# Second expert group's gates made first, groups of 76 and 52, and first-stage products kept in PSUM banks

## The chip, the cores and the metric

One NeuronCore of one Trainium2 chip runs the kernel in one launch. The metric is device time of that launch in microseconds. Engines are called as the profile calls them: PE multiplies matrices, DVE and ACT work on tiles of up to 128 partitions, POOL does the same more slowly, SP issues the loads. "mmb" and "msb" are PSUM banks (128 x 512 f32), everything else lies in SBUF.

## What is computed

Two transformer blocks over 256 tokens of width 1024, all in f32. The first block is a pair of convolution mixers, a cross-attention to 256 memory rows, and a layer of 16384 small experts; the second is attention and an MLP. The change concerns the mixers and the experts:

```
sc_b, sc_c, sc_x, cf_a, cf_g, gate_sc, gate_cf = jnp.split(h @ w_in, cuts)
y_sc = sc_b * causal_depthwise_conv(sc_c * sc_x, sc_conv_w)     # 3 taps
cf   = causal_depthwise_conv((cf_a + b) * sigmoid(cf_g + b), cf_conv_w)  # 31 taps
...
top_s, top_i = lax.top_k(sub_scores, 16)          # 8 heads, two halves of 128 keys
cand = top_s[0][:, None] + top_s[1][None, :]      # 256 candidates
fin_s, fin_pos = lax.top_k(cand, 16)              # 16 experts of each head
gates = softmax(fin_s)
act = gelu(u[expert] . h) * gates
out = sum over experts of act * v[expert]
```

## The kernel before

Activations lie transposed (features on partitions, 256 tokens along a row). f32 precision comes from splitting: every weight tile `w` (128 x 1024, 512 KB, loaded by SP into one of three buffers) is split by ACT into `wh` (L288) and by POOL or DVE into `wl` = w - wh (L292), and a **unit** is 24 matmuls of 128 x 256 (L370): `wh` with the high and the low part of the activation, `wl` with the high part. What follows a unit (`post_...`) reads its mmb bank.

The order on all engines comes from a planner, `Sched`, at build time. Work is written as generators of `Op(engine, cost, fn, deps, ev)`; the planner keeps a clock for each engine, adds each `Op`'s planned cost, and emits what is due while it walks the units in PE's order. `sch.need(events)` emits work until the events are planned. An engine runs its queue in that order, so a cost in the table moves instructions and a `need` puts what follows behind what it asked for.

The stages around the change:

- **First stage** (0 to about 290 us): units of `w_in` in columns a, g (the 31-tap mixer `cf`) and c, x, b (the 3-tap mixer `sc`). DVE runs `cf`'s taps with one SCALAR_TENSOR_TENSOR each (L607, accumulating in an msb bank). `post_x` makes the 3-tap filter: `scx` = x * c (L238), then one TENSOR_SCALAR (L659) and two SCALAR_TENSOR_TENSORs (L662) in the SBUF tile `scy`; `post_b` multiplies `scy` into b's bank and splits the result into `eA`, `eB`, the activations of later units. `prep_n` and `prep_mem` make the normalised `hN` and `memHL` over an SBUF tile `mt` (L238, L479).
- **U**: 128 units of `peer_u`; unit n's 128 experts are multiplied with h. `post_u` writes gelu to `Ah[n // 64][:, n % 64]` (L1239, ACT).
- **Choice**: during the first third of U, `topk_head` and then `select(t)` for the two halves of 128 tokens run on DVE. In `select`, four quarters of is_equal, multiply and reduce (L1179, L1182, L1185) turn positions to expert numbers; three PE transposes (L1192), ACT copies (L1196, L1200) and two DVE operations (L1201, L1203) give `sel`: for each of a token's 128 chosen experts the unit number i (0 to 127), the row j in the unit and the gate g.
- **Gates**: `gbatch(hh, t0)` makes the gates of 8 tokens for one group `hh` of units. DVE: J (L1255, is_equal, 128 x 1024 f16), I (L1259, is_equal, 8 tokens x 64 units), T (L1262, I times g in two parts). PE: 8 matmuls J x T (L1274) into two msb banks. For each bank, ACT copies the low part out (L1284), DVE adds it (L1286) and multiplies the sum into `Ah[hh]` (L1288). Two lanes take 16 batches each (`gate_lane`). Group 0 (units 0 to 63) runs during units 64 to 127; group 1 during the first half of V.
- **V**: 128 units of `peer_v`, in the order 0 to 127, accumulated in four msb banks (L1362, L1364, L1366). `z_split` turns gated activations into `zz`: high part by ACT (L241), low part by DVE (L238); it needs all 32 batches of the unit's group. At V's 72nd unit the rope angles of the second block are spawned on DVE (`angles`, `distances`).

Of the kernel before, what the change touches and what calls it, by code (L numbers as in the profile page):

```python
# [200 lines left out]
def tile_kernel(ctx, tc, A, out):  # L201
# [449 lines left out]
    def post_x(j):  # L651
        def g(p):
# [32 lines left out]
    def prep_n(k):  # L685
        t = T1.tile([128, S], F32, tag="mt", bufs=2, name="mt")
# [18 lines left out]
    def layer_norm():  # L705
# [122 lines left out]
    for key, j in order:  # L828
        u_in[key, j] = add(W["w_in"][tiles0[key] + j])
# [19 lines left out]
    u_V = [add(W["peer_v"][n]) for n in range(128)]  # L849
# [288 lines left out]
    def top16(val, idx, src, tmp, n, ev=None, deps=()):  # L1138
        yield Op("dve", c_dve(n), lambda: V.max(val[:, 0:8], src), deps=deps)
        yield Op("dve", c_dve(n), lambda: V.max_index(idx[:, 0:8], val[:, 0:8], src), chain=False)  # L1140
        yield Op("dve", c_dve(n), lambda: V.match_replace(tmp, val[:, 0:8], src, LOW), chain=False)
        yield Op("dve", c_dve(n), lambda: V.max(val[:, 8:16], tmp))
        yield Op("dve", c_dve(n), lambda: V.max_index(idx[:, 8:16], val[:, 8:16], tmp), ev=ev)

    def topk_head(h):
        for t in range(2):
# [9 lines left out]
    def select(t):  # L1156
# [14 lines left out]
        yield Op("dve", c_dve(128), lambda: V.tensor_scalar(FQ[:, 0], fp, 4, None, op0=OP.logical_shift_right))  # L1171
        yield Op("dve", c_dve(128), lambda: V.tensor_copy(AFi[:, t], FQ[:, 0]))
        yield Op("dve", c_dve(128), lambda: V.tensor_scalar(FQ[:, 1], fp, 15, None, op0=OP.bitwise_and))
        yield Op("dve", c_dve(128), lambda: V.tensor_copy(BFi[:, t], FQ[:, 1]))
        for q, (pos, dst) in enumerate(((AFi, IF), (BFi, JF))):
            for c in range(2):
                eq = EQ[c].rearrange("p (s r) -> p s r", r=16)
                eq4 = EQ[c].rearrange("p (h s r) -> p h s r", h=4, r=16)
# [953 lines left out]
```

## Time and profile before

| | |
|---|---|
| runs | 1784.63, 1784.19, 1780.41 us; median 1784.19 |
| profiled execution | 1783.02 us, span 1781.2 us, 1.8 us around it |
| busy share of the span | PE 90%, PEld 89%, DVE 76%, POOL 68%, ACT 47% |
| granted TensorE clock, mean | 0.951 |

The span runs from the first to the last instruction. Busy shares are means over stages that differ, so the stretches below are read one by one. A clock of 1.00 is 2.4 GHz, 0.50 is 1.2 GHz. In a wait, the engine named first sat idle until the instruction after the arrow ended.

### The profile page before, as it was taken

How to read it: one execution, taken by the hardware profiler on the slowest of the kernel's cores; microseconds unless marked ns; L12 is line 12 of the kernel's file. 1: busy time of each engine (PE TensorE's matmuls, PEld its weight loads, DVE VectorE, ACT ScalarE, POOL GpSimd, SP SyncE). 2: the span in 40 equal slices, each digit the busy share in tenths (PEclk: the TensorE clock that was granted, in tenths of full speed). 3: DMA queues.
4: the chain of work that ended last, by engine and by line, in shares of the span. 5: the costliest groups of instructions: out<-in, count | busy, mean ns of one | idle time of the engine just before them, and what ended most of it. 6: DMA issues, size and time to landing. Idle time of an engine off the chain costs nothing. (4 is left out here: it accounts for less than half of the span.)

```text
span 1781.2 us, 32465 instructions
## 1 busy us (share of the span) xinstructions
PE 1605.8 (90%) x12948; PEld 1579.4 (89%) x12948; DVE 1362.3 (76%) x2122; ACT 839.0 (47%) x1431; POOL 1210.3 (68%) x509
## 2 busy tenths in 40 slices
PE   8898988898997899999988888878999889979997
PEld 7898988898997899999888888878999779979997
DVE  7999966758899805999999999978887886464302
ACT  5533445555443444444444334333455455556533
POOL 5677865546687787777766666646887533758885
PEclk8999999999998999999999989988999899989999
DMA  5444544434354354444443434333555322535553
GB/s 202 155 166 154 193 155 140 154 125 151 134 187 154 119 189 151 158 145 156 157 153 131 137 118 142 138 108 137 179 187 169 119 80 72 179 129 179 188 185 113
DMA packets 75304, 266.69 MB, mean 150 GB/s; under 512 B 8720, under 2 KB 9232, under 8 KB 75152
## 3 DMA queue, kind: packets, MB, share of 16 engines
q1 hardware_dynamic: 73856, 262.77, 43.3%
q8 instruction: 101, 1.65, 0.4%
q10 hardware_dynamic: 1296, 1.85, 0.3%
q14 instruction: 51, 0.42, 0.1%
HBM read 262.48 MB, written 2.10 MB: 149 GB/s over the span
## 5 line engine op out<-in xcount | busy, mean ns | idle before, releaser
L292 POOL TENSOR_TENSOR wl<-w,wh 128x1024 fp32r<-128x1024 f32 x473 | 1186.6, 2514 | 539.8 <-ACT wh L288 437.5
L288 ACT ACTIVATE wh<-w 128x1024 fp32r<-128x1024 f32 x491 | 518.2, 1058 | 499.0 <-PE mmb L370 152.6
L1364 PE MATMUL msb<-zz,wh 128*128 128x256 f32 x1008 | 260.0, 293 | 6.9 <-DVE zz L238 6.8
L1362 PE MATMUL msb<-zz,wh 128*128 128x256 f32 x1008 | 260.8, 293 | 3.0 <-ACT zz L241 3.0
L370 PE MATMUL mmb<-hA,wh 128*128 128x256 f32 x1024 | 256.9, 288 | 0.0
L370 PE MATMUL mmb<-hB,wh 128*128 128x256 f32 x1024 | 254.9, 286 | 0.0
L238 DVE TENSOR_TENSOR zz<-Ah,zz 128x256 fp32r<-128x256 f32 x128 | 215.8, 1689 | 35.1 <-ACT zz L241 35.1
L1364 PEld LDWEIGHTS msb<-zz,wh 128*128 128x128 f32 x1008 | 203.6, 202 | 8.1 <-DVE zz L238 8.1
L1362 PEld LDWEIGHTS msb<-zz,wh 128*128 128x128 f32 x1008 | 203.6, 202 | 3.4 <-ACT zz L241 3.4
L370 PEld LDWEIGHTS mmb<-hA,wh 128*128 128x128 f32 x1024 | 199.4, 195 | 0.0
L370 PEld LDWEIGHTS mmb<-hB,wh 128*128 128x128 f32 x1024 | 199.2, 195 | 0.0
L1366 PE MATMUL msb<-zz,wl 128*128 128x256 f32 x1008 | 149.1, 292 | 0.0
L370 PE MATMUL mmb<-hA,wl 128*128 128x256 f32 x1024 | 146.3, 286 | 0.0
L1366 PEld LDWEIGHTS msb<-zz,wl 128*128 128x128 f32 x1008 | 135.8, 200 | 0.0
L370 PEld LDWEIGHTS mmb<-hA,wl 128*128 128x128 f32 x1024 | 133.2, 193 | 0.0
L370 PE MATMUL mmb<-hN,wh 128*128 128x256 f32 x896 | 118.7, 284 | 12.7 <-ACT hN L241 5.5
L370 PEld LDWEIGHTS mmb<-hN,wh 128*128 128x128 f32 x896 | 111.9, 194 | 14.5 <-ACT wh L288 5.9
L607 DVE SCALAR_TENSOR_TENSOR msb<-glu,vec,msb 128x256 f32<-128x256 f32 x232 | 113.0, 487 | 6.2
L1274 PEld LDWEIGHTS <-ohF 128*128 128x128 f16 x512 | 38.7, 151 | 71.3 <-DVE selT L1262 41.3
L1259 DVE TENSOR_TENSOR ohF<-selT 128x512 f16<-128x512 f16 x64 | 98.9, 1545 | 0.0
L1255 DVE TENSOR_TENSOR ohF<-selT 128x1024 f16<-128x1024 f16 x64 | 80.9, 1265 | 0.0
L1262 DVE TENSOR_TENSOR ohF<-ohF,selT 128x1024 f16<-128x1024 f16 x32 | 79.1, 2473 | 0.1
(478 smaller groups left out, 3285.7 us busy)
## 6 DMA issues: line engine op xcount, KB each, us to landing
w<-in_peer_u_dram SPq DMA_DIRECT2D x128, 512.0 KB, 3.2
w<-in_peer_v_dram SPq DMA_DIRECT2D x128, 512.0 KB, 3.2
w<-in_w_in_dram SPq DMA_DIRECT2D x81, 512.0 KB, 3.3
w<-in_w_up_dram SPq DMA_DIRECT2D x32, 512.0 KB, 3.7
w<-in_w_down_dram SPq DMA_DIRECT2D x32, 512.0 KB, 4.3
w<-in_w_peer_q_dram SPq DMA_DIRECT2D x16, 512.0 KB, 3.5
w<-in_w_v_dram SPq DMA_DIRECT2D x8, 512.0 KB, 3.2
w<-in_sc_w_out_dram SPq DMA_DIRECT2D x8, 512.0 KB, 4.3
```

The lines of the kernel that those rows point to most:

```text
L238: return lambda e="dve": ENG[e].tensor_tensor(o, a, b, op=op)
L288: yield Op("act", c_act(1024), lambda: ACT.activation(h, w, AF.Copy), deps=u["wdep"], ev=("H", u["i"]))
L292: lambda e: ENG[e].tensor_tensor(l, w, h.bitcast(F32), op=OP.subtract), ev=("L", u["i"]))
L370: PE.matmul(p[:, :S], a, b, start=first and n == 0, stop=last and n == len(todo) - 1)
L607: lambda k=k: V.scalar_tensor_tensor(cc[:, j] if k == 30 else o(), glu[:, j, k:k + S], vcol("cf_w", j * 31 + k), o(), op0=OP.mult, op1=OP. ...
L1255: yield Op("dve", G_J, lambda: V.tensor_tensor(ohJ, iotax, sel["j"][:, None, sl].to_broadcast([128, 128, 8]), op=OP.is_equal), deps=[("sel ...
L1259: yield Op("dve", G_I, lambda: V.tensor_tensor(ohI, iotan[:, None, hh * 64:(hh + 1) * 64].to_broadcast([128, 8, 64]), sel["i"][:, sl][:, : ...
L1262: yield Op("dve", G_T, lambda: V.tensor_tensor(gT, ohI[:, :, None].to_broadcast([128, 8, 2, 64]), sel["g"][:, :, sl].rearrange("p a t -> p ...
L1274: PE.matmul(banks[c][:, t * 128:(t + 1) * 128], ohJ[:, :, 4 * c + t], gT[:, 4 * c + t], start=True, stop=True, skip_group_check=True)
L1362: PE.matmul(o, u["H"][:, d, :], opH, start=first and d % 2 == 0, stop=False, skip_group_check=True)
L1364: PE.matmul(o, u["H"][:, d, :], opL, start=False, stop=False, skip_group_check=True)
L1366: PE.matmul(o, u["L"][:, d, :], opH, start=False, stop=last, skip_group_check=True)
```

## The change

Three things, in one diff of some 500 lines.

**Groups.** The units are split 76 and 52. The gates of group 1 (units 76 to 127) are made first, as soon as both halves of `sel` are planned and at the latest before unit 48; they need no activation, so one DVE addition stores them in `Ah[1]` (L1328 of the new kernel). From unit 76 on, `post_u` runs gelu in the bank and one DVE operation multiplies it with the kept gate (L1264). Before unit 76, `sch.need` asks for all of group 1's batches; then group 0's start, in chunks of 3, 3 and 2 tokens. V takes units 76 to 127 first, then 0 to 75. Between the start of the gates and unit 76, the `wl` splits are held on DVE by a bias (units 51 to 75). Banks for gates rotate over four.

**First stage.** `prep_n`, `prep_mem` and the first two steps of the 3-tap filter write into PSUM banks; only the last tap writes SBUF. The `wl` of all `w_in` tiles are held on POOL.

**Costs.** The planner's costs of DVE operations on SBUF rise by 1050 ns in `select`, `z_split` and the angles (`c_wait`), and some other costs are set to other numbers.

```diff
+def c_wait(n, ap=0, fast=False):
+
+    return 1050 + c_dve(n, ap, fast)
...
     def prep_mem(k):
-        t = T1.tile([128, S], F32, tag="mt", bufs=2, name="mt")
+        t = prep_bank[k % 2]()[:, :S]
...
-            yield Op("dve", c_dve(S), tt(b[:, 2:2 + S], p[:, :S], scc[j], OP.mult), deps=[("scc", j)])
-            yield Op("dve", c_dve(S, 1, True),
-                     lambda: V.tensor_scalar(y, b[:, 0:S], vcol("sc_w", j * 3), None, op0=OP.mult))
+
+            o = p[:, :S]
+            yield Op("dve", c_psum(S), tt(b[:, 2:2 + S], o, scc[j], OP.mult), deps=[("scc", j)])
+            yield Op("dve", c_psum(S, 2),
+                     lambda: V.tensor_scalar(o, b[:, 0:S], vcol("sc_w", j * 3), None, op0=OP.mult))
             for k in (1, 2):
-                yield Op("dve", c_dve(S, 1),
-                         lambda k=k: V.scalar_tensor_tensor(y, b[:, k:k + S], vcol("sc_w", j * 3 + k), y,
-                                                            op0=OP.mult, op1=OP.add),
+                yield Op("dve", c_psum(S, 1),
+                         lambda k=k: V.scalar_tensor_tensor(y if k == 2 else o, b[:, k:k + S],
+                                                            vcol("sc_w", j * 3 + k), o, op0=OP.mult, op1=OP.add),
                          ev=("scy", j) if k == 2 else None)
...
-        u_in[key, j] = add(W["w_in"][tiles0[key] + j])
+        u_in[key, j] = add(W["w_in"][tiles0[key] + j], bias=-1e6)
...
+    NG = (76, 52)
+    vord = list(range(NG[0], 128)) + list(range(NG[0]))
+    u_V = [add(W["peer_v"][n]) for n in vord]
...
     def post_u(n):
+        g_, m = place(n)
+
         def g(p):
-            yield Op("act", c_act(S), lambda: ACT.activation(Ah[n // 64][:, n % 64], p[:, :S], AF.Gelu),
-                     ev=("U", n))
+            if g_ == 0:
+                yield Op("act", c_act(S), lambda: ACT.activation(Ah[0][:, m], p[:, :S], AF.Gelu), ev=("U", n))
+                return
+
+            a, z = p[:, :S], Ah[1][:, m]
+            yield Op("act", c_act(S), lambda: ACT.activation(a, a, AF.Gelu))
+            yield Op("dve", c_psum(S), lambda: V.scalar_tensor_tensor(
+                z, a, 1.0 / GS, z, op0=OP.mult, op1=OP.mult), deps=[("Z", 1, 240), ("Z", 1, 248)], ev=("U", n))
...
+    def gbank(key):
+
+        if len(gbanks) >= 4:
+            sch.need([gbanks[-4]])
+        gbanks.append(key)
+        return gpool[0]()
...
+        chunks = [(t, min(per, 8 - t)) for t in range(0, 8, per)]
...
+            if hh == 1:
+                yield Op("dve", c_psum(nt * NI), lambda view=view, lc=lc, z=z: V.tensor_tensor(
+                    z, view(0), lc, op=OP.add), deps=[("Ga", hh, t0, c)], chain=False, ev=("Zc", hh, t0, c))
+                continue
...
-        if n == 64:
-            sch.need([("U", 62), ("sel", 0), ("sel", 1)])
-            Ah[1] = P2.tile([128, 64, S], F32, tag="A1", name="Ah1")
+        if Ah[1] is None and (n == 48 or n > 4 and ("sel", 0) in sch.ev and ("sel", 1) in sch.ev):
+            sch.need([("sel", 0), ("sel", 1)])
+            Ah[1] = P2.tile([128, NG[1], S], F32, tag="A1", name="Ah1")
             ohF[0] = epool.tile([128, 4096], HF, tag="e0a", name="ohF")
-            sch.need([("U", 63)])
-            gates_half(0, msb)
+            ACT.activation(iotan(), iota, AF.Copy)
+            gates_group(1)
+
+            for k in range(n + 3, NG[0]):
+                u_U[k]["bias"] = 1e6
+        if n == NG[0]:
+            sch.need([("U", NG[0] - 1)] + [("Z", 1, t0) for t0 in range(0, 256, 8)])
+            gates_group(0)
...
-        if n == 72:
+        if n == NG[1] + 4:
```

In the first stage, DVE's order around one filter of the 3-tap mixer reads before:

```order
L607 SCALAR_TENSOR_TENSOR msb<-glu,vec,msb 128x256 x6
L238 TENSOR_TENSOR scx<-mmb,scc 128x256
L659 TENSOR_SCALAR scy<-scx,vec 128x256
L607 SCALAR_TENSOR_TENSOR msb<-glu,vec,msb 128x256
L662 SCALAR_TENSOR_TENSOR scy<-scx,vec,scy 128x256
L607 SCALAR_TENSOR_TENSOR msb<-glu,vec,msb 128x256
L662 SCALAR_TENSOR_TENSOR scy<-scx,vec,scy 128x256
L238 TENSOR_TENSOR mmb<-mmb,scy 128x256
```

and now, with the bank of x (mmb) as the place of the running sum:

```order
L620 SCALAR_TENSOR_TENSOR msb<-glu,vec,msb 128x256 x6
L248 TENSOR_TENSOR scx<-mmb,scc 128x256
L674 TENSOR_SCALAR mmb<-scx,vec 128x256
L677 SCALAR_TENSOR_TENSOR mmb<-scx,vec,mmb 128x256
L620 SCALAR_TENSOR_TENSOR msb<-glu,vec,msb 128x256
L677 SCALAR_TENSOR_TENSOR scy<-scx,vec,mmb 128x256
L248 TENSOR_TENSOR mmb<-mmb,scy 128x256
```

The three filter operations are the same, on other operands; a tap of the other mixer (L607, now L620) has moved out from between the first and the second.

In U, PE's order at the first half's transposes of `select` (L1192) reads before, after 33 units (the second half's follow in the same way after 42.67 units):

```order
L370 MATMUL mmb<-hA,wh 128x256
L370 MATMUL mmb<-hB,wh 128x256
L370 MATMUL mmb<-hA,wl 128x256 x8
L1192 MATMUL msb<-cst,scr 128x128 x3
L370 MATMUL mmb<-hA,wh 128x256
L370 MATMUL mmb<-hB,wh 128x256
```

and now, after 48 units:

```order
L380 MATMUL mmb<-hA,wh 128x256
L380 MATMUL mmb<-hB,wh 128x256
L380 MATMUL mmb<-hA,wl 128x256 x8
L1210 MATMUL msb<-cst,scr 128x128 x6
L380 MATMUL mmb<-hA,wh 128x256
L380 MATMUL mmb<-hB,wh 128x256
```

Both halves' transposes now stand behind unit 47 with no unit between them. On DVE the second half's chain stands behind the first half's last two operations (L1219, L1221, which read the transposes), as before:

```order
L1200 TENSOR_TENSOR scr<-scr 128x1024
L1203 TENSOR_REDUCE scr<-scr 128x64
L1219 SCALAR_TENSOR_TENSOR scr<-msb,selT 128x128
L1221 CAST selT<-scr 128x128
L1179 TENSOR_TENSOR scr<-scr 128x128
L1183 TENSOR_REDUCE scr<-scr 128x8
L1184 RECIPROCAL scr<-scr 128x8
```

Behind it on DVE come group 1's batches, the first ones among the `wl` splits of units 51 to 75 (L302; J is L1294, I L1298, T L1301, the addition into `Ah` L1328):

```order
L1221 CAST selT<-scr 128x128
L1294 TENSOR_TENSOR ohF<-selT 128x1024
L302 TENSOR_TENSOR wl<-w,wh 128x1024
L1298 TENSOR_TENSOR ohF<-ohF,selT 128x416
L1294 TENSOR_TENSOR ohF<-selT 128x1024
L302 TENSOR_TENSOR wl<-w,wh 128x1024
L1301 TENSOR_TENSOR ohF<-ohF,selT 128x832
L302 TENSOR_TENSOR wl<-w,wh 128x1024
L1298 TENSOR_TENSOR ohF<-ohF,selT 128x416
L302 TENSOR_TENSOR wl<-w,wh 128x1024
L1328 TENSOR_TENSOR Ah_7162<-msb,hT 128x52x4 x2
L1301 TENSOR_TENSOR selT<-ohF,selT 128x832
```

The last `wl` on DVE belongs to unit 75. Then batch follows batch with no unit's work between, as in these rows:

```order
L1301 TENSOR_TENSOR ohF<-ohF,selT 128x832
L1294 TENSOR_TENSOR ohF<-selT 128x1024
L1298 TENSOR_TENSOR ohF<-ohF,selT 128x416
L1328 TENSOR_TENSOR Ah_7162<-msb,hT 128x52x4 x2
L1301 TENSOR_TENSOR selT<-ohF,selT 128x832
L1294 TENSOR_TENSOR ohF<-selT 128x1024
L1298 TENSOR_TENSOR ohF<-ohF,selT 128x416
L1328 TENSOR_TENSOR Ah_7162<-msb,accp 128x52x4
L1301 TENSOR_TENSOR ohF<-ohF,selT 128x832
L1328 TENSOR_TENSOR Ah_7162<-msb,selT 128x52x4
```

Eleven of the 32 batches have their matmuls on PE between units 52 and 76; those of the other 21 (168 matmuls) stand in one piece after unit 75, ahead of unit 76. Of group 0's batches 20 have their matmuls between units 78 and 126, one where U ends, 10 in V's units 2 to 26. Before, each half of U and V had 32 batches spread over 60 units.

## Rows read from the trace of the kernel before

**Rows 1.** Stretches: length, busy us and instructions of each engine, PEclk, DMA share, GB/s.
```profile
88.80:186.50 97.70, 88.92 (x736) 85.94 (x736) 91.45 (x166) 38.53 (x54) 74.36 (x39) 1.00 0.48 162
474.80:633.60 158.80, 141.71 (x1155) 141.02 (x1154) 139.08 (x357) 70.73 (x109) 126.04 (x47) 0.95 0.46 158
633.60:679.70 46.10, 46.10 (x387) 46.10 (x386) 0.00 (x0) 21.34 (x34) 37.48 (x16) 1.00 0.54 184
723.30:900.20 176.90, 164.38 (x1432) 161.21 (x1432) 171.78 (x181) 83.34 (x156) 135.93 (x51) 1.00 0.44 152
900.60:1172.40 271.80, 221.95 (x1793) 216.77 (x1793) 262.42 (x289) 107.50 (x194) 170.34 (x65) 0.91 0.38 132
1160.00:1172.40 12.40, 3.25 (x25) 2.51 (x25) 10.77 (x22) 2.80 (x8) 0.00 (x0) 0.50 0.11 40
1172.40:1177.00 4.60, 4.60 (x20) 4.43 (x21) 1.38 (x4) 1.35 (x4) 0.00 (x0) 0.50 0.00 0
1172.40:1363.80 191.40, 184.96 (x1478) 184.38 (x1479) 157.82 (x103) 87.56 (x129) 145.66 (x61) 0.95 0.48 164
```

**Rows 2.** Waits of PE over the span: us in total, times, longest.
```profile
PE mmb L1274 <- DVE selT L1262: 34.4, 13, 4.9
PE msb L1192 <- DVE scr L1185: 17.1, 3, 9.7
...
PE mmb L370 <- ACT wh L288: 7.1, 6, 2.2
```

**Rows 3.** Timeline of PE at two first-stage waits: start, length, idle before, releaser.
```profile
154.66 2.10 PE L370 MATMUL mmb<-hN,wh 128*128 128x256 f32 x16 [1.13 <-ACT wh L288]
...
164.92 2.15 PE L370 MATMUL mmb<-hN,wh 128*128 128x256 f32 x16 [1.16 <-ACT wh L288]
```

**Rows 4.** DVE groups, 0 to 230: count, busy us, mean ns, idle before.
```profile
L607 DVE SCALAR_TENSOR_TENSOR msb<-glu,vec,msb 128x256 f32<-128x256 f32 x214 | 104.3, 487 | 5.9
L662 DVE SCALAR_TENSOR_TENSOR scy<-scx,vec,scy 128x256 f32<-128x256 f32 x16 | 19.8, 1240 | 0.0
L659 DVE TENSOR_SCALAR scy<-scx,vec 128x256 f32<-128x256 f32 x8 | 11.5, 1436 | 0.9
...
L603 DVE TENSOR_SCALAR msb<-glu,vec 128x256 f32<-128x256 f32 x8 | 4.4, 546 | 0.3
...
L717 DVE TENSOR_TENSOR msb<-cc 128x256 f32<-128x256 f32 x1 | 1.4, 1402 | 0.0
```

**Rows 5.** Timeline of DVE in a quarter of select.
```profile
577.60 1.23 DVE L1182 TENSOR_TENSOR scr<-scr 128x1024 f32<-128x1024 f32 x1
```

**Rows 6.** Timeline of DVE in the last gate batches.
```profile
1160.05 1.21 DVE L1262 TENSOR_TENSOR selT<-ohF,selT 128x1024 f16<-128x1024 f16 x1
...
1161.52 0.67 DVE L1255 TENSOR_TENSOR ohF<-selT 128x1024 f16<-128x1024 f16 x1
...
1162.75 0.68 DVE L1259 TENSOR_TENSOR ohF<-selT 128x512 f16<-128x512 f16 x1
1163.35 0.42 DVE L1288 SCALAR_TENSOR_TENSOR Ah<-mmb,Ah 128x256 f32<-128x256 f32 x1
...
1167.82 1.21 DVE L1262 TENSOR_TENSOR selT<-ohF,selT 128x1024 f16<-128x1024 f16 x1
```

**Rows 7.** DVE groups, 707 to 900, gates beside POOL's splits.
```profile
L1255 DVE TENSOR_TENSOR ohF<-selT 128x1024 f16<-128x1024 f16 x27 | 44.7, 1657 | 0.0
L1259 DVE TENSOR_TENSOR ohF<-selT 128x512 f16<-128x512 f16 x27 | 43.1, 1596 | 0.0
L1262 DVE TENSOR_TENSOR ohF<-ohF,selT 128x1024 f16<-128x1024 f16 x13 | 42.0, 3230 | 0.0
...
L1262 DVE TENSOR_TENSOR selT<-ohF,selT 128x1024 f16<-128x1024 f16 x14 | 19.0, 1358 | 0.5
```

**Rows 8.** POOL's splits in the same stretch.
```profile
L292 POOL TENSOR_TENSOR wl<-w,wh 128x1024 fp32r<-128x1024 f32 x56 | 148.9, 2659 | 49.5 <-ACT wh L288 49.2 <-DMA w<-in_peer_u_dram 0.3
```

**Rows 9.** DVE group of the lo part of zz, 900 to 1172.
```profile
L238 DVE TENSOR_TENSOR zz<-Ah,zz 128x256 fp32r<-128x256 f32 x64 | 84.2, 1317 | 3.3 <-ACT zz L241 3.3
```

More of the change, by code (lines that the diff above doesn't have):

```diff
@@ L80, in __init__ @@
         self.cos = []
+        self.busy = []
     def spawn(self, gen, prio=0.0, ready=None):
@@ L109, in emit @@
         op = co.op
+        self.busy.append(co)
         if isinstance(op.eng, str):
@@ L113, in emit @@
             op.fn(eng)
+        self.busy.remove(co)
         self.vt[eng] = st + cost
@@ L127, in pick @@
         for co in self.cos:
+            if co in self.busy:
+                continue
             e = self.est(co)
@@ L1265, in gbatch, with f @@
             op=OP.mult), ev=("Gi", hh, t0))
-        lo = ((hT[:, 0], hT[:, 1]), (RpD[:, :S], acc2[:, :]))[q]
-        banks = [None, None]
-        def f(c):
+        chunks = [(t, min(per, 8 - t)) for t in range(0, 8, per)]
+        banks = {}
+        def f(c, ts, nt):
             def g():
-                banks[c] = pool()
-                for t in range(4):
-                    PE.matmul(banks[c][:, t * 128:(t + 1) * 128], ohJ[:, :, 4 * c + t], gT[:, 4 * c + t],
+                banks[c] = gbank(("Zc", hh, t0, c))
+                for t in range(nt):
+                    PE.matmul(banks[c][:, t * 2 * NI:(t + 1) * 2 * NI], ohJ[:, :, ts + t], gT[:, ts + t],
@@ L1275, in g @@
                               start=True, stop=True, skip_group_check=True)
             return g
-        for c in range(2):
-            yield Op("pe", 4 * 85.0, f(c), chain=c == 0, ev=("Gp", hh, t0) if c else ("Gc", hh, t0))
-        for c in range(2):
-            view = lambda i, c=c: banks[c].rearrange("p (t a i) -> p a i t", t=4, a=2)[:, i]
-            lc = lo[c].rearrange("p (i t) -> p i t", t=4)
-            z = Ah[hh][:, :, t0 + 4 * c:t0 + 4 * c + 4]
-            yield Op("act", 380.0, lambda view=view, lc=lc: ACT.activation(lc, view(1), AF.Copy),
-                     deps=[("Gp", hh, t0) if c else ("Gc", hh, t0)], chain=False, ev=("Ga", hh, t0, c))
-            yield Op("dve", c_psum(256), lambda view=view, lc=lc: V.tensor_tensor(view(0), view(0), lc, op=OP.add),
+        last = len(chunks) - 1
@@ new lines, in gbatch @@
+        for c, (ts, nt) in enumerate(chunks):
+            yield Op("pe", nt * (25 + NI), f(c, ts, nt), chain=c == 0,
+                     ev=("Gp", hh, t0) if c == last else ("Gc", hh, t0, c))
+        for c, (ts, nt) in enumerate(chunks):
+            view = lambda i, c=c, nt=nt: banks[c][:, :nt * 2 * NI].rearrange("p (t a i) -> p a i t", t=nt, a=2)[:, i]
+            lc = lo[q][c][:, :nt * NI].rearrange("p (i t) -> p i t", t=nt)
+            z = Ah[hh][:, :, t0 + ts:t0 + ts + nt]
+            yield Op("act", 140.0 + 0.94 * nt * NI, lambda view=view, lc=lc: ACT.activation(lc, view(1), AF.Copy),
+                     deps=[("Gp", hh, t0) if c == last else ("Gc", hh, t0, c)], chain=False, ev=("Ga", hh, t0, c))
+            if hh == 1:
+                yield Op("dve", c_psum(nt * NI), lambda view=view, lc=lc, z=z: V.tensor_tensor(
+                    z, view(0), lc, op=OP.add), deps=[("Ga", hh, t0, c)], chain=False, ev=("Zc", hh, t0, c))
+                continue
+            yield Op("dve", c_psum(nt * NI), lambda view=view, lc=lc: V.tensor_tensor(view(0), view(0), lc, op=OP.add),
@@ L1300, in gate_lane, with iotan, gates_group @@
-    def gate_lane(hh, off, pool):
+                ev=("Zc", hh, t0, c))
+        yield Op("dve", 0.0, lambda: None, ev=("Z", hh, t0))
+    def iotan():
+        return ohF[0][:, 3872:4000]
+    def gates_group(hh):
+        for t0 in (-16, -8):
+            for key in ("Gp", "Gi"):
+                sch.ev[(key, hh, t0)] = 0.0
+        for off in (0, 8):
+            sch.spawn(gate_lane(hh, off), prio=300.0)
+    def gate_lane(hh, off):
         for t0 in range(off, 256, 16):
-            yield from gbatch(hh, t0, pool)
+            yield from gbatch(hh, t0)
```

146 lines of the change are left out of this document (74 added, 72 removed).

## The prediction

> **What bounds the kernel now.** I read the stretches first, cut at the starts of the gelu of units 0, 48, 64 and 76 and at V's first matmul, so that every stage has a length of its own [rows 1]. Between 633.6 and 679.7, where DVE has nothing to do, PE is busy throughout: 16 units in 46.1 us, 2.88 each. That is the floor of a unit in U and V, and what a stage takes above it is the loss. U from unit 76 on takes 176.9 for 52 units; DVE is busy for 171.8 of it, so the gates on DVE set the pace there. V's first 64 units take 271.8 against 64 x 2.88 = 184.3; DVE is busy for 262.5. V's rest takes 191.4 for 62 units (178.6). The waits name what PE stood for [rows 2]: 34.4 us in V for T, 17.1 in U for `select`.
>
> The groups then show why DVE is slow. With POOL idle at V's last batches (POOL 0.00 in 1160 to 1172.4 [rows 1]) J takes 0.67, I 0.68 and T 1.21 us [rows 6]; beside POOL's splits, 2.66 us each [rows 8] (2.34 with DVE idle: 37.48 for 16 [rows 1]), J means 1.66, I 1.60, T 1.36 and 3.23 [rows 7]. I read that as waiting for POOL's current split: about 1 us for each operation that reads two SBUF tiles. The first stage shows the same by operand: the filter's TENSOR_SCALAR into SBUF takes 1436 ns, the mixer's into a bank 546; the filter's taps in SBUF 1240, the mixer's, which read a bank, 487 [rows 4].
>
> **The change part by part** (against the span of 1781.2; 1.8 us lie around it, and this execution is 1.2 us under the median of the runs).
>
> *First stage.* The filter's TENSOR_SCALAR falls to the price of its like into a bank, the taps to that of taps that read one: 8 x (1.44 - 0.55) + 16 x (1.24 - 0.49) = 19 us less DVE work. DVE was busy for 91.5 of 97.7 us in this stage [rows 1], and PE's waits lie 10.26 us apart (154.66 and 164.92 [rows 3]) where three units of 24 matmuls would take 8.16 (736 matmuls in 83.4, at the 2.72 us that units take between waits). Behind the wait stands `wh`, but what is late is `eA`, `eB` and the filter ahead of it, through which the units and their buffers are held. DVE's work in a period, 91.5/97.7 x 10.26 = 9.6, loses 19/8 = 2.4 and comes under PE's 8.16. I take 8.3, since taps and filter still follow each other on one queue: seven periods lie between eight filters, 7 x 1.96 = 13.7. The floor allows 97.7 - 83.4 = 14.3, the bound above. The bound below is 0: `wl`, now on POOL alone, takes 2.34 to 2.66 us of each 2.72 [rows 1, 8], with a memset beside it. In the new order the layer norm's sums come later behind the taps: +1. Products of `mt` that read two SBUF tiles gain nothing by going to a bank: the one such operation in the trace, `msb<-cc`, took 1402 ns although its result goes to a bank [rows 4]. Net **-13**.
> The Trainium skill says in "VectorE: DVE Perf Modes", section "Why PSUM operands drop a tier", that an operand in PSUM bars DVE's two-port mode for f32. By that rule alone the filter's TENSOR_SCALAR would get slower, this part would bring nothing and the time would be about 1782; what the rows show beside a busy POOL (1436 in SBUF, 546 into a bank) goes the other way. "SBUF — State Buffer", section "Who interferes with whom", says that two SBUF inputs contend with POOL's reads, one input does not; the rows agree (1402 against 487).
>
> *Start of U to unit 48.* Before: 158.8 us, of which 17.1 waits for `select`. Now the transposes of both halves stand behind unit 47. The first half's chain is in its last quarter at 577.60 [rows 5], well ahead of PE; the second half's cannot start until PE has done the first half's, so all of it lies bare: four quarters of 3 x 1.22 = 3.65 us (1.23 us for a 1024-wide operation [rows 5]; POOL is soon idle, its buffers full), and an estimate of 5 to 7 for a dozen small operations of at most 0.42, the transposes and the copies: some 21. DVE's work of the second half, which was hidden behind ten units, is what stands open. 48 x 2.88 + 22 = 160.2: **+1.5**. If POOL's waits of 1 us met each of the twelve large operations, it would be 12 more: bound +13.
>
> *Units 48 to 75.* Before 723.3 - 633.6 = 89.7 us. Now 28 units, 80.6, and the 11 batches' matmuls between them: 25 of them took 3.25 at half clock, so 8 take 0.5 at full: 6. DVE has 25 `wl` of some 1.2 (as wide and of the same type as the row of 1.23 [rows 5]) and 11 batches of 3 us here, 63 of 87 us, so PE should stand little. Then 21 batches bare, with PE and POOL idle. A batch of group 1 on DVE: J 0.65, I 0.68 x 416/512 = 0.55, T 1.21 x 832/1024 = 1.0, two additions of 0.42 less a fifth, 0.7 [rows 6]: 2.95. 21 x 2.95 = 62. Behind the last such wait, in which PE was busy for 3.25 of 12.4 us, the granted clock was 0.50 (1.2 GHz) for 4.6 us more [rows 1]: 2.3 lost. 80.6 + 6 + 62 + 2 = 150.6: **+61**. Bounds of a batch: 2.6 (operations overlap at their ends: I of 0.68 at 1162.75, the next at 1163.35) and 3.9, the pace of V's last batches (7.77 for two, 1160.05 to 1167.82).
>
> *Units 76 to 127.* Before 176.9 with some 26 batches; now 20 to 21, but larger: DVE J 0.6, I 0.75, T 1.35, three additions and three multiplications 1.6, the gate's multiplication of 2.4 units 0.8, together 5.1, and the waits for POOL. Those were 1.0 for J, 0.9 for I and 1.1 for T: 3.0 a batch [rows 7], with POOL 77% busy as it will be. PE has 2.43 x 2.88 + 0.5 = 7.5. The two engines' exclusive time, splits and two-input operations, is 2.43 x 2.34 + 2.7 = 8.4. I take 8.6 x 21 = 180.6: **+4**. Bounds 8.0 (-9) and 10 (+33).
>
> *V.* Before 463.2 us for 126 units. Now the units of group 1 need no gates, and only 10 batches run, in V's first 26 units. 126 x 2.88 = 362.9; 10 x 0.5 = 5; exclusive time of a batch in V is 2.4 x 2.34 + 2.7 + 2.4 x 0.42 (the low part of zz, 1.32 with waits [rows 9], priced as a bank operation without) = 9.3 against 7.4 on PE: 10 x 1.9 = 19 lost; V's rest lost 12.8 with the angles in it, which now go one by one between zz: 7 with the clock. 362.9 + 5 + 19 + 7 = 394, and 2 for V's start: 396: **-67**. Bounds of the loss: 5 and 45 (32 batches lost 70 to 88).
>
> Sum: -13 + 1.5 + 61 + 4 - 67 = -13.5. 1783.0 - 13.5 = 1769.5, say **1769**. The two large terms nearly cancel: the bare gates cost what V gets back.
>
> **Rivals.** (1) *Slower: the bare batches go at the pace of V's last ones.* A batch's matmuls wait for T, its copy for the matmuls, its addition for the copy, and four banks hold but two batches; PE at half clock and ACT would then set the pace. For it: 3.9 us in that drain, with PE at 0.50 and DVE idle for 1.6 of 12.4 us [rows 1]. Against: those batches hold four bank operations of 0.42, the new two. It decides from (13.5 + 5.4)/21 = 0.9 more, 3.85 a batch; at 4.1 it adds 24: 1793. (2) *No change: the first stage keeps its period.* POOL, which alone splits now, takes up to 2.66 for each of three tiles, 8.0 of 8.16, and with memsets and any wait for DVE it is the bound. Then -1 stands for -13: 1781. Against: at 2.34 it has room. (3) *Larger gain: batches overlap.* 2.6 us bare (-7), and V's 10 batches lose 10 instead of 21: 1752. For it: in V POOL has slack once zz waits for no group. That the bank edit does nothing is ruled out for the filter by the pairs of [rows 4]; for `mt` it is what I count.
>
> **The numbers.** 5.4 us, 0.3%, is what can be told from no change. Forecast (1757 to 1778) 0.46, larger gain 0.16, slower 0.18, no change 0.20, of which a part lies under 1778.8. Faster 0.64, same 0.18, slower 0.18. For 8 in 10 the range runs from the larger gain to past the slower rival: 1751 to 1796. The likeliest case's own range is 1757 to 1778.
>
> **What would show it.** PE waits for `sel` once, some 20 us after unit 47; a stretch of some 60 us with PE and POOL idle ahead of unit 76, at clock 0.50; V's first 64 units in some 215 us instead of 271.8; the filter's TENSOR_SCALAR near 546 ns and first-stage waits for `wh` gone or 8.3 us apart. I am wrong if the bare batches take 3.9 or more, if units 51 to 75 stand for DVE's `wl` behind gates that wait for PE (1 us each is +24), or if the stage of the mixers is as long as before.

## The result, and the profile after

The changed kernel takes 1758.1 us (median of 1760.9, 1758.68, 1757.51 and 1753.83) against 1783.33 for the kernel before: a ratio of 0.9859, 95% interval 0.9835 to 0.9883, so 25 us or 1.4% faster. The forecast was 1769 and faster. The profiled execution took 1760.9 us (span 1759.1), 22.1 less than that of before.

Cut at the same places (starts of the gelu of units 0, 48 and 76, V's first matmul and the end of its last), the two profiled executions differ like this:

| stretch | before | after | difference | forecast |
|---|---|---|---|---|
| start to unit 0 | 474.8 | 452.5 | -22.3 | -13 |
| unit 0 to 48 | 158.8 | 160.6 | +1.8 | +1.5 |
| unit 48 to 76 | 89.7 | 145.3 | +55.6 | +61 |
| unit 76 to V | 177.3 | 190.0 | +12.7 | +4 |
| V (900.6 to 1371.0; 948.4 to 1351.9) | 470.4 | 403.5 | -66.9 | -67 |
| rest | 410.2 | 407.2 | -3.0 | 0 |

The sum is -22.1. The two large terms of the groups, with the smaller ones beside them, add up to +3; what the kernel gained in these two executions stands ahead of U. Two rows hang on the execution of before that was profiled: three kernels below that leave U as it was (pool_only, filter_only, first_only) took 162.8 to 163.0 us from unit 0 to 48 where it took 158.8, and the old first stage ended at 467.3 and 468.7 in two others (pool_only, groups_only) where it ended at 474.8.

The stretches of the changed kernel, as in [rows 1]: length, busy time and instructions of PE, PEld, DVE, ACT, POOL, then clock, DMA share, GB/s.

```profile
88.80:186.50 97.70, 97.70 (x856) 97.70 (x855) 86.74 (x185) 46.41 (x63) 86.46 (x43) 1.00 0.60 196
452.50:613.10 160.60, 141.22 (x1156) 140.72 (x1156) 127.34 (x368) 71.16 (x110) 124.07 (x48) 0.94 0.49 159
613.10:696.40 83.30, 83.26 (x728) 82.58 (x726) 63.53 (x81) 40.51 (x75) 4.80 (x2) 1.00 0.51 170
696.40:758.40 62.00, 24.19 (x194) 20.12 (x195) 59.47 (x108) 16.91 (x47) 2.82 (x1) 0.53 0.03 10
753.30:758.40 5.10, 5.10 (x26) 5.10 (x26) 4.68 (x5) 2.20 (x4) 2.82 (x1) 0.50 0.07 10
758.40:948.40 190.00, 168.79 (x1392) 164.41 (x1392) 165.49 (x234) 85.70 (x167) 133.16 (x51) 0.97 0.44 144
948.40:1060.00 111.60, 92.09 (x730) 89.92 (x731) 108.19 (x126) 44.90 (x87) 71.80 (x27) 0.92 0.41 133
1060.00:1344.60 284.60, 284.60 (x2373) 284.60 (x2373) 246.83 (x146) 139.25 (x206) 237.06 (x100) 1.00 0.56 183
```

In 88.8 to 186.5 PE is now busy throughout and does 856 matmuls where it did 736. From 613.1 to 696.4 it is busy throughout too, beside the first eleven batches. Then come 62.0 us, unit 76 at half clock at their end, in which PE does 24 us of work at a clock of 0.53 and POOL 2.8: the 21 bare batches, those with no unit's matmuls beside them. V runs without a gap from 1060 on.

What PE waited for, of the changed kernel over the span; the row for T in V and that for `select` answer to [rows 2]:

```profile
PE msb L1313 <- DVE selT L1301: 30.4, 12, 2.9
PE msb L1313 <- DVE ohF L1301: 20.7, 19, 2.9
PE msb L1210 <- DVE scr L1203: 19.4, 2, 12.6
```

The waits for T (L1301) are now mostly those of the bare stretch (37.7 of the 51.1 us). The wait for `select` is 19.4 us in two pieces, against 17.1 in three.

DVE's groups of the first stage, of the changed kernel, as in [rows 4]:

```profile
L248 DVE TENSOR_TENSOR msb<-mem,Rm 128x256 f32<-128x256 f32 x8 | 7.8, 1014 | 0.0
...
L677 DVE SCALAR_TENSOR_TENSOR mmb<-scx,vec,mmb 128x256 f32<-128x256 f32 x8 | 3.9, 490 | 0.3
L674 DVE TENSOR_SCALAR mmb<-scx,vec 128x256 f32<-128x256 f32 x8 | 3.9, 488 | 1.1 <-POOL scx L669 0.3
...
L677 DVE SCALAR_TENSOR_TENSOR scy<-scx,vec,mmb 128x256 f32<-128x256 f32 x8 | 3.8, 475 | 0.0
L489 DVE SCALAR_TENSOR_TENSOR hN<-msb,vec,hN 128x256 fp32r<-128x256 f32 x8 | 3.7, 475 | 0.0
```

The filter's TENSOR_SCALAR fell from 1436 to 488 ns and its taps from 1240 to 490 and 475. The gain operation of `hN`, which reads the product from a bank, takes 475. The product itself still reads two SBUF tiles and gained nothing: 1014 ns into the bank. Before, from and into SBUF, the two read:

```profile
L479 DVE SCALAR_TENSOR_TENSOR hN<-mt,vec,hN 128x256 fp32r<-128x256 f32 x8 | 10.4, 1329 | 0.0
...
L238 DVE TENSOR_TENSOR mt<-mem,Rm 128x256 f32<-128x256 f32 x8 | 5.7, 741 | 0.0
```

DVE's groups of the bare stretch, 697 to 758.4:

```profile
L1294 DVE TENSOR_TENSOR ohF<-selT 128x1024 f16<-128x1024 f16 x22 | 14.9, 683 | 0.0
L1298 DVE TENSOR_TENSOR ohF<-ohF,selT 128x416 f16<-128x416 f16 x20 | 11.7, 586 | 0.3
L1301 DVE TENSOR_TENSOR ohF<-ohF,selT 128x832 f16<-128x832 f16 x10 | 10.2, 1023 | 0.3
...
L1328 DVE TENSOR_TENSOR Ah<-msb,hT 128x208 f32<-128x208 f32 x21 | 7.2, 371 | 0.5 <-ACT hT L1325 0.5
```

0.68 + 0.59 + 1.02 + 2 x 0.37 = 3.0, and ends overlap a little. The stretch is 62.0 us; unit 76's own matmuls take 5.1 of it (753.3 to 758.4) at a clock of 0.50, 1.2 GHz. That leaves 56.9 for 21 batches, 2.71 each.

### The profile page after: what moved, and what is told of

It is laid out like the page before. It is cut to its first block, busy times and chain, and to the rows that moved or that the text cites. A ratio compares the mean times of both kernels' runs of the same rounds, so it can differ in the third digit from the quotient of the medians.

```text
span 1759.1 us, 32653 instructions
## 1 busy us (share of the span) xinstructions
PE 1587.0 (90%) x12948; PEld 1562.7 (89%) x12948; DVE 1336.5 (76%) x2197; ACT 848.8 (48%) x1463; POOL 1140.9 (65%) x486
## 4 chain that ended last, share of the span: by engine, by line
PE 65%; DVE 27%; issue 3%; ACT 3%; DMA 1%; POOL 1%; SPq 0%; DVEq 0%; ACTq 0%; POOLq 0%
PE mmb L380 35%; PE msb L1423 8%; PE msb L1425 8%; PE msb L1421 8%; DVE msb L620 3%; DVE ohF L1301 3%; DVE ohF L1298 3%; DVE zz L248 1%; DVE ohF L1294 1%; DVE selT L1301 1%; ACT wh L298 1%; DVE Ah L1333 1%; DVE wl L302 1%; PE msb L1313 1%; DVE prT L1740 1%
## 5 line engine op out<-in xcount | busy, mean ns | idle before, releaser
L302 POOL TENSOR_TENSOR wl<-w,wh 128x1024 fp32r<-128x1024 f32 x451 | 1117.6, 2482 | 588.7 <-ACT wh L298 514.8
L248 DVE TENSOR_TENSOR zz<-Ah,zz 128x256 fp32r<-128x256 f32 x128 | 256.9, 2010 | 37.3 <-ACT zz L251 35.8
L1423 PE MATMUL msb<-zz,wh 128*128 128x256 f32 x1008 | 251.1, 286 | 3.5 <-DVE zz L248 3.5
L1421 PE MATMUL msb<-zz,wh 128*128 128x256 f32 x1008 | 251.1, 286 | 0.8 <-DVE Ah L1333 0.8
L1423 PEld LDWEIGHTS msb<-zz,wh 128*128 128x128 f32 x1008 | 193.9, 192 | 3.7 <-DVE zz L248 3.7
L1421 PEld LDWEIGHTS msb<-zz,wh 128*128 128x128 f32 x1008 | 194.0, 192 | 0.9 <-ACT zz L251 0.9
L1425 PE MATMUL msb<-zz,wl 128*128 128x256 f32 x1008 | 144.3, 286 | 0.0
L1425 PEld LDWEIGHTS msb<-zz,wl 128*128 128x128 f32 x1008 | 131.3, 192 | 0.0
L620 DVE SCALAR_TENSOR_TENSOR msb<-glu,vec,msb 128x256 f32<-128x256 f32 x232 | 113.2, 488 | 6.4
L302 DVE TENSOR_TENSOR wl<-w,wh 128x1024 fp32r<-128x1024 f32 x40 | 63.9, 1599 | 33.2 <-ACT wh L298 31.4
L380 PE MATMUL mmb<-eu,wh 128*128 128x256 f32 x512 | 72.9, 292 | 5.6 <-DVE uHL L484 2.6
L1298 DVE TENSOR_TENSOR ohF<-ohF,selT 128x416 f16<-128x416 f16 (+1 forms) x64 | 77.7, 1214 | 0.3
```

Source lines behind the costliest of these rows:

```text
L248: return lambda e="dve": ENG[e].tensor_tensor(o, a, b, op=op)
L302: lambda e: ENG[e].tensor_tensor(l, w, h.bitcast(F32), op=OP.subtract), ev=("L", u["i"]))
L380: PE.matmul(p[:, :S], a, b, start=first and n == 0, stop=last and n == len(todo) - 1)
L620: lambda k=k: V.scalar_tensor_tensor(cc[:, j] if k == 30 else o(), glu[:, j, k:k + S], vcol("cf_w", j * 31 + k), o(), op0=OP.mult, op1=OP. ...
L1298: yield Op("dve", 400.0 + 8 * NI, lambda: V.tensor_tensor(ohI, iotan()[:, None, i0:i0 + NI].to_broadcast([128, 8, NI]), sel["i"][:, sl][:, ...
L1421: PE.matmul(o, u["H"][:, d, :], opH, start=first and d % 2 == 0, stop=False, skip_group_check=True)
```

## The experiments

Each ran beside the kernel before on one chip; the ratio is to that. Where a stage is given, it is of one profiled execution. Start to unit 0 itself differs by a few us between executions (448 to 454 in kernels with the new filter; 467 to 475 in those with the old), so within-stage times are read from unit 0 on.

**Which part gained: first_only and groups_only.** The diff is taken apart at the first stage (banks for `mt` and the filter, `w_in`'s splits held on POOL).

> The kernel before with the first-stage part alone: products and filter sums in banks, all w_in splits on POOL. U starts 22.3 us earlier in the changed kernel (452.5 against 474.8). Theory 1: all of the gain is the first stage, and the groups cancel: -22 to -25, about 1760. Theory 2: the stage gives the forecast 13, the rest of its gain comes from the new planner costs, and the groups give some 10: about 1770.

Measured: 1761.6 us, ratio 0.9886 (0.9863 to 0.9910), 20 us less: theory 1 within the interval, not theory 2. U starts at 452.55, as in the changed kernel.

> The changed kernel with the first stage of before: mt and the filter in SBUF, the planner free to choose who splits w_in. Theory 1: no change, 1780 to 1784. Theory 2: 1773 or less.

Measured: 1774.0 us, ratio 0.9975 (0.9954 to 0.9996). Neither theory quite: the groups and the costs give something, 4.4 us with an interval of 0.7 to 8.2 by the ratio, 8.7 by the medians (1782.71 for the kernel before beside it), too little to hold them for the cause and not nothing.

Where it lies can be read from the traces of groups_only and pool_only, which both have the old filter: from unit 0 on, stage by stage as in the table, -2.5, +54.9, +12.3, -69.0 and -0.8, together -5. (U starts 1.4 us later in groups_only, in spite of the next 3 us: further ahead its profiled execution was some 4 us slower.) Some 3 us lie just ahead of U, in matmuls that the diff leaves as they were. From the last matmul of the 16 units before U (mmb<-pe0a) to the gelu of unit 0 it is 6.9 us in groups_only and in the changed kernel, and 9.8 to 10.4 in before, pool_only, filter_only and first_only. PE waits there 0.3 us for `pqF` with the new costs and 1.5 to 1.9 with the old ones, and over the last 11.7 us its granted clock is 1.00 in groups_only, 0.71 before and 0.85 in filter_only.

**Which part of the first stage: filter_only and pool_only.** The first part of the diff, with the two taps behind it, is filter_only; it changes the operands and the planner's costs of the same operations. The second part, at both places where such tiles are added, is pool_only.

```diff
+            o = p[:, :S]
-            yield Op("dve", c_dve(S, 1, True), lambda: V.tensor_scalar(y, b[:, 0:S], ...
+            yield Op("dve", c_psum(S, 2), lambda: V.tensor_scalar(o, b[:, 0:S], ...
...
-        u_in[key, j] = add(W["w_in"][tiles0[key] + j])
+        u_in[key, j] = add(W["w_in"][tiles0[key] + j], bias=-1e6)
```

> The kernel before, only the 3-tap filter's sums moved into x's bank. If waits for POOL on the filter were the price, 19 us less DVE work: -12 to -18, the period near 8.2 us. If the splits' move to POOL is needed too, -5 or less.

> The kernel before, only the w_in splits held on POOL. Five splits of 1.2 us leave DVE and take 2.4 on POOL. If DVE's work is what counts, -3 to 0; if POOL becomes the bound of the stage, +3 or more; if the splits on DVE were the price, -8 or more.

Measured: filter_only 1758.2 us, ratio 0.9872 (0.9850 to 0.9895); pool_only 1780.5, 0.9988 (0.9970 to 1.0007). The filter's 24 operations alone bring all that the first stage brought, 23 us (19 to 27) and so more than the 12 to 18 expected. Moving the splits brings nothing that can be told (2 us, -1 to 5), and neither do the banks for `mt`. The filter's two groups, and the stretch, in filter_only:

```profile
L664 DVE SCALAR_TENSOR_TENSOR mmb<-scx,vec,mmb 128x256 f32<-128x256 f32 x8 | 3.9, 490 | 0.3
L661 DVE TENSOR_SCALAR mmb<-scx,vec 128x256 f32<-128x256 f32 x8 | 3.9, 488 | 0.9
```

```profile
88.80:186.50 97.70, 97.70 (x856) 97.70 (x856) 88.02 (x189) 47.87 (x65) 87.97 (x43) 1.00 0.60 200
```

The same 856 matmuls in 97.7 us as in the changed kernel. PE's waits behind that stretch, first before (186.5 to 290), then in filter_only (80 to 290):

```profile
PE mmb L370 <- ACT hN L241: 5.5, 1, 5.5
PE mmb L370 <- DVE gs L238: 4.8, 1, 4.8
PE msb L724 <- DVE accl L717: 1.8, 1, 1.8
```

```profile
PE mmb L370 <- ACT hN L241: 5.4, 1, 5.4
...
PE msb L726 <- DVE accl L719: 1.4, 1, 1.4
```

The wait for `hN` stands in both. The wait of 4.8 us for `gs` has gone: DVE reached the end of the taps late before, and PE stood for what came behind them.

**Whether a bare batch costs its DVE time: gate_costs.**

```diff
-        yield Op("dve", 1000.0, lambda: V.tensor_tensor(
+        yield Op("dve", 680.0 if hh == 1 else 1000.0, lambda: V.tensor_tensor(
             ohJ, iotax, ...
```

> The changed kernel, with planner costs of group 1's J, I and T at 680, 530 and 970 instead of 1000, 816 and 1332: the same operations, but 15 instead of 11 batches stand between units 48 and 76, and 17 instead of 21 bare ahead of unit 76. Theory (a bare batch costs its DVE time, 2.8 us; DVE has 20 of 85 us free in units 48 to 75): the bare stretch 11 us shorter, units 48 to 75 +2 for the matmuls, sum -9. Rival (the stretch before unit 76 is full, a batch added there costs the same): 0.

Measured: 1752.0 us, ratio 0.9835 (0.9800 to 0.9871). Units 48 to 75 and the bare stretch:

```profile
613.50:700.40 86.90, 85.49 (x757) 84.49 (x756) 72.81 (x100) 42.52 (x84) 5.51 (x2) 1.00 0.53 169
700.40:751.70 51.30, 20.36 (x162) 17.12 (x163) 49.55 (x87) 13.99 (x37) 2.82 (x1) 0.53 0.01 2
```

The bare stretch fell by 10.7 us for four batches, 2.7 each; units 48 to 75 took 3.6 more. That is the theory, at -7 for both and not -9. The kernel as a whole gained less: beside the changed kernel's profiled execution units 76 to V were 3 us shorter and V 5 longer, for a reason that no run shows, and the two ratios to before (0.9835 and 0.9859) do not tell the kernels apart. The reading rests on the stages.

**Whether the splits had to go to DVE: splits_on_pool.** The loop that sets the bias is left out.

> The changed kernel without the bias that holds the splits of units 51 to 75 on DVE; 19 batches come to stand between units 48 and 76, 13 bare. Theory (an operation with two SBUF inputs waits some 1 us for POOL): a batch there takes 5.9 us of DVE, 19 of them 112 us against 83, +25 to +30; bare stretch -23; sum +2 to +7. Rival (the bias is not needed): -15 to -20.

Measured: 1763.5 us, ratio 0.9892 (0.9852 to 0.9931). Units 48 to 75 and the bare stretch, then the gates' groups there, then the same groups in the changed kernel:

```profile
610.30:714.00 103.70, 92.34 (x792) 90.05 (x790) 103.24 (x92) 44.86 (x92) 69.87 (x27) 0.97 0.42 137
714.00:754.00 40.00, 15.76 (x131) 13.37 (x132) 38.46 (x69) 11.36 (x31) 2.67 (x1) 0.57 0.04 14
```

```profile
L1294 DVE TENSOR_TENSOR ohF<-selT 128x1024 f16<-128x1024 f16 x18 | 34.1, 1892 | 0.0
L1301 DVE TENSOR_TENSOR ohF<-ohF,selT 128x832 f16<-128x832 f16 x10 | 24.7, 2472 | 0.2
```

```profile
L1294 DVE TENSOR_TENSOR ohF<-selT 128x1024 f16<-128x1024 f16 x11 | 8.8, 798 | 0.0
...
L1301 DVE TENSOR_TENSOR ohF<-ohF,selT 128x832 f16<-128x832 f16 x6 | 6.1, 1020 | 0.0
```

With the splits on POOL, J takes 1.89 us instead of 0.80 and T 2.47 instead of 1.02, and DVE is busy for 103.2 of 103.7 us; the bare stretch is 22 us shorter, units 48 to 75 20 longer. The work on POOL beside the gates is what makes them slow; this run changes it and leaves the gates' operations as they were. The two stretches together came 2 us shorter than in the changed kernel, where the theory had +2 to +7; the rival's -15 to -20 did not come. So the bias makes the gates fast there, but in these stages it saves no time. The kernel as a whole is 5 us slower than the changed one by the medians; in the profiled executions that lies in V (408 us against 403), which is not explained.

**Why the second half of sel lay bare: first_sel_at_40, then exp_earlier.** In the changed kernel DVE's timeline in `select` reads:

```profile
553.95 0.29 DVE L1183 TENSOR_REDUCE scr<-scr 128x8 f32<-128x128 f32 x1 [19.45 <-ACT scr L251]
...
555.17 2.32 DVE L1190 CAST scr<-scr 128x128 f32<-128x128 uint32 x1
...
559.06 3.31 DVE L1200 TENSOR_TENSOR scr<-scr 128x1024 f32<-128x1024 f32 x1
...
582.50 1.22 DVE L1203 TENSOR_REDUCE scr<-scr 128x64 f32<-128x1024 f32 x1
587.41 0.29 DVE L1219 SCALAR_TENSOR_TENSOR scr<-msb,selT 128x128 f32<-128x128 f32 x1 [3.69 <-ACT selT L1218]
...
591.28 0.23 DVE L1190 CAST scr<-scr 128x128 f32<-128x128 uint32 x1
...
593.07 1.23 DVE L1200 TENSOR_TENSOR scr<-scr 128x1024 f32<-128x1024 f32 x1
...
605.27 1.22 DVE L1203 TENSOR_REDUCE scr<-scr 128x64 f32<-128x1024 f32 x1
```

DVE stood for 19.45 us until ACT had done an exponential (L251) that the planner had put behind the 36th gelu. The first half's chain then ran beside POOL (L1200 3.31 us) and ended at 583.7, some 2.5 us before PE came to its transposes. The second half's ran with POOL idle (L1200 1.23 us), 587.4 to 606.5, and PE stood.

```diff
+        if n == 40:
+            sch.need([("sel", 0)])
```

> The changed kernel with one more need: the first half of sel is asked for ahead of unit 40, so its transposes stand behind unit 39 and not behind unit 47; the second half stays at 48. Theory: DVE stood idle from 534.5 to 554.0 for an ACT operation that the order had put late, and the second half's chain then runs beside units 40 to 47: of some 20 us of waiting at unit 48 five to ten are left, perhaps 3 appear at unit 40: -10 to -16. Rival (the chain beside POOL takes 31 us as before, and both halves' waits remain): -3 to +2.

Measured: 1760.0 us, ratio 0.9902 (0.9868 to 0.9935). No gain: 2 us more than the changed kernel by the medians, the rival's size, and 8 by the ratios, for another reason than the rival's. The row of DVE in that kernel, and PE's wait:

```profile
549.77 0.28 DVE L1183 TENSOR_REDUCE scr<-scr 128x8 f32<-128x128 f32 x1 [19.46 <-ACT scr L251]
```

```profile
PE msb L1210 <- DVE scr L1203: 20.3, 3, 8.5
```

The need had not moved the exponential: the planner's costs for `top16` put it there. PE now stood for 20.3 us in three pieces instead of two. The next kernel moves the exponential.

```diff
-        yield Op("dve", 155 + 1.06 * n, lambda: V.max(val[:, 0:8], src), deps=deps)
+        yield Op("dve", 1.0 * c_dve(n), lambda: V.max(val[:, 0:8], src), deps=deps)
...
+        if n == 40:
+            sch.need([("sel", 0)])
-        if Ah[1] is None and (n == 48 or
+        if Ah[1] is None and (n == 51 or
```

> The changed kernel with cheaper planner costs for top16 (c_dve(n) instead of 155 + 1.06 n), a need for the first half of sel ahead of unit 40, and unit 51 instead of 48 for both halves. select's exponential moves on ACT from behind the 36th gelu of U to behind the 28th, the second half's from the 48th to the 41st; 23 batches instead of 21 stand bare. Theory (the 19.5 us in which DVE waits for that exponential are what leaves the second half's chain bare): waits for sel fall from 19.4 to 3 to 8, two bare batches cost 5.6: -6 to -11. Rival (the chains themselves are too long; PE stands for them wherever the transposes are): waits of 15 or more, 0 to +6.

Measured: 1750.9 us, ratio 0.9848 (0.9808 to 0.9887). DVE's rows, the last two the ends of the two chains, and PE's wait:

```profile
530.39 0.29 DVE L1183 TENSOR_REDUCE scr<-scr 128x8 f32<-128x128 f32 x1 [0.38 <-ACT scr L251]
...
563.35 1.22 DVE L1203 TENSOR_REDUCE scr<-scr 128x64 f32<-128x1024 f32 x1
...
600.05 1.22 DVE L1203 TENSOR_REDUCE scr<-scr 128x64 f32<-128x1024 f32 x1
```

```profile
PE msb L1210 <- DVE scr L1203: 6.0, 2, 3.0
```

0.38 us of waiting instead of 19.45, 6.0 us of PE's time instead of 19.4. From unit 0 to unit 76 the kernel takes 296.2 us against 305.9, two more bare batches included. The cost put back, c_dve(n), is the one that the kernel before had, where the two exponentials stand behind the 25th and the 33rd gelu: it was the change's own new cost for `top16` that put the first of them late. By the ratios (0.9848 and 0.9859) this kernel is not told apart from the changed kernel; by the medians it is 7 us faster. The waits are the theory's, but three things changed at once, and the exponential is not the whole of it. Counted from the gelu of unit 0, the first half's chain ended 17.3 us earlier than in the changed kernel (113.9 against 131.2), the second half's only 3.4 earlier (150.6 against 154.0), since it now ran beside POOL (its four multiplications took 3.3 us each and not 1.23). PE, for its part, came to the second half's transposes 13.6 us later, 8.6 of them for the three units more. In first_sel_at_40, which has the changed kernel's costs, the second half's chain ended at 157.1; PE's waits there were 11.7 us at unit 40 and 8.5 at unit 48. Asked for at unit 51 it would have had the 11.7 alone: an estimate from these rows, no run has it. By it the exponential is worth some 6 of the 13.4 us, and the place of the needs the rest.

**Both together: sel_and_costs, exp_and_costs, exp_and_low_costs.**

> Both together, with costs of 500, 400 and 700: 18 batches between units 48 and 76, 14 bare. Theory: -10 to -16 for sel, bare stretch -20, units 48 to 75 a few us longer since DVE is full there: -25 to -30, about 1730. Rival: units 48 to 75 give back what the stretch saves: -10 to -16.

Measured: 1745.7 us, ratio 0.9793 (0.9758 to 0.9828). The theory's 1730 did not come; the time is the rival's, but again not for its reason. The need at 40 was no help by itself (163.2 us from unit 0 to 48 against 160.6), so the gain is that of the lower costs, 14 batches bare instead of 21: 294.3 us from unit 0 to 76 against 305.9. The bare stretch is 42.0 us instead of 62.0, and units 48 to 75 give back 5.8 of these 20 (89.1 against 83.3).

> The same with J, I, T at 680, 530, 970 in the planner: 19 batches bare instead of 23. Theory: 11 us off the bare stretch, some 3 back in units 51 to 75, as with the costs alone: about 1740. Rival: as before, 1750 or more.

> The same with 500, 400, 700: 16 batches bare. Units 54 to 75 then hold 16 batches of 2.8 us and 22 splits of 1.2, 71 us of DVE in 63 of PE, so DVE sets the pace there. Theory: bare stretch 20 us shorter than with 23, units 51 to 75 some 8 to 10 longer: 1736 to 1742, little less than with 680, 530, 970. Rival (the stalls are spread and cost no more than bare batches do): the same as those.

Measured: 1740.1 us, ratio 0.9772 (0.9747 to 0.9798), and 1740.9 us, 0.9779 (0.9745 to 0.9812). From unit 51 to 75 and the bare stretch, of the first, then of the second:

```profile
604.40:681.10 76.70, 76.69 (x679) 75.93 (x678) 64.64 (x86) 37.29 (x74) 7.60 (x3) 1.00 0.52 166
681.10:734.50 53.40, 21.31 (x179) 17.66 (x180) 52.37 (x98) 15.28 (x42) 2.73 (x1) 0.55 0.03 10
```

```profile
605.80:685.00 79.20, 78.75 (x704) 77.69 (x703) 72.55 (x101) 38.84 (x79) 5.40 (x3) 1.00 0.49 161
685.00:733.00 48.00, 19.06 (x155) 16.04 (x155) 46.48 (x83) 13.22 (x36) 2.82 (x1) 0.54 0.03 11
```

Both times are as expected. The lower costs take 5.4 us off the bare stretch and put 2.5 on units 51 to 75; the medians cannot tell the two apart. They are 41 and 40 us, 2.3 and 2.2%, faster than the kernel before, and 14 to 18 faster than the changed one (by the ratios and by the medians).

## Why the prediction was right, step by step

**Sign and place.** Faster was forecast and came, 11 us beyond the forecast and inside its range. Its terms put -13 on the first stage and -0.5 on everything else; first_only, filter_only and groups_only show that this is where the gain lies, with 4.4 us (0.7 to 8.2) for the rest. The errors of the terms partly cancel: the first stage was off by -9, units 48 to 76 by -5 and the end of the kernel by -3 (it takes 407 to 410 us in the kernels here), unit 76 to V by +9. So that the time lies well inside the range is in part luck. Rival 3's time, 1752, is nearer to the measured one than the forecast, but of its two reasons only the shorter batches came.

**First stage: -13 forecast, -22.3 read; by their ratios first_only gains 20 and filter_only 23.** The mechanism was right (waits of the filter for POOL, 1436 to 488 and 1240 to 490), and the stretch that I looked at came as sized: 120 more matmuls in 97.7 us is 13.7 us of PE work, what the period of 8.3 us gave, near the bound of 14.3. But I looked at one stretch only, and that is the step that failed here: the 4.8 us for `gs` behind it hung on the same backlog of DVE and went too, which was not in the sum. The charge of +1 for the layer norm was 0.7 (2.5 us for `accl` against 1.8). Of the 4.5 us that this leaves some 3.5 lie just ahead of unit 0 (10.4 us before, 6.9 after); groups_only has them and filter_only has not, so they come with the groups and the new costs, and the sum had nothing for them. (filter_only starts U as early without them; it is some 3 us quicker between 330 and 440, in stages that its edit does not touch.) Rival 2, the bound of POOL, fell with pool_only and with POOL's 86.5 us of 97.7. That the products of `mt` gain nothing was right for the products (1014 after 741) and wrong for the operation behind them (1329 to 475); at the end it made no time, as filter_only shows. The reading that an operation waits when it reads two SBUF tiles is too narrow: the filter's TENSOR_SCALAR reads one (`scx`) and took 1436 ns into SBUF and 488 into a bank. The rule of the Trainium skill, "VectorE: DVE Perf Modes", section "Why PSUM operands drop a tier", would have had the filter slower by itself; no run here shows that, and beside POOL it became faster.

**Unit 0 to 48: +1.5, read +1.8.** The wait of 19.4 us came as worked out, and the stage took 160.6 us where 160.2 were forecast. That the difference agrees too is luck: against the 162.8 to 163.0 of the other kernels with the old order it would be -2.3. What lay ahead of the wait I had not seen: 19.45 us of DVE idle in the first half's chain, which exp_earlier takes away.

**Unit 48 to 76: +61, read +55.6.** A bare batch took 2.71 us against 2.95, 5 us over the 21; the 11 batches between units were hidden, and the clock took the 2 us that were counted, as 5.1 for unit 76 instead of 2.9. Rival 1, batches bound by one another's waits, fell: DVE was busy for 59.5 of the 62.0 us.

**Unit 76 to V: +4, read +12.7.** Here the mechanism failed. I took DVE and its waits for POOL as the bound, 8.6 us a batch; with the 21 batches it was 9.0, and DVE was busy for 165.5 of 190.0 us only, so it was not the bound all the time. PE's waits there:

```profile
PE msb L1313 <- DVE ohF L1301: 10.2, 9, 1.1
PE msb L1313 <- DVE Ah L1333: 7.1, 13, 0.7
```

All in all it waited 20.4 us there, against 12.2 before. Thirteen of these waits are for the last multiplication into `Ah` of a batch before, which frees one of four banks where a batch now takes three, and 2.7 us more lie at the join of U and V. That the banks are the cause was not tried.

**V: -67, read -66.9.** The number is luck in part. Up to 1060 V did 26.75 units (730 matmuls less 88 for the gates) in 111.6 us, 34.6 above the floor of 2.88 each, where 26 were forecast. The forecast counted 10 batches there; it is 11, since of the 32 only 21 stand before V. Behind them V runs at the floor, 284.6 us without a gap, where 7 us of loss were forecast. The two errors cancel.

## What to carry to other kernels

Price an operation by which of its operands lie in SBUF while the other engine on that memory is busy: moving a running sum into a bank that was free anyway gave more here than rearranging the largest stage. When two large terms cancel, look at what stands bare in the new stretch, and at the planner's costs that put it there: costs taken from the trace moved four batches under cover, 7 us net up to unit 76, and one new cost had put an exponential so late that DVE stood for it for 19 us. And follow the backlog of a slow engine past the stretch that it slows; the wait behind it goes as well.

## What was not expected of the hardware

The TENSOR_SCALAR with its result in a bank took 488 ns, the mixer's of the same shape 546. And the wait of an operation for POOL can be nearly a whole split of 2.3 to 2.7 us: `select`'s multiplication of two SBUF tiles took 3.31 us beside POOL and 1.23 without, a CAST of 128 columns, which reads one tile, 2.32 and 0.23.
